# Low weight parts by an accumulating DMA: every fourth ordinary block of a two-layer trunk

## The chip, the cores and the metric

The kernel runs on one NeuronCore of a Trainium2 chip. Five engines work side by side, each through its own queue of instructions in order: TensorE (PE in the profile, its weight loads PEld), VectorE (DVE), ScalarE (ACT), GpSimd (POOL) and SyncE (SP). Sixteen DMA engines move data between DRAM (HBM) and the on-chip memory SBUF. Instructions wait for each other through semaphores.

The metric is the device time of one execution in microseconds (us). The kernel before took 2592.8 us, the median of three runs from 2591.97 to 2593.14.

## The reference

The reference is a decoder trunk with two layers (`DEPTH = 2`), 256 tokens and a width of 2048, in float32. Layer 0 mixes tokens by retention, layer 1 by a short gated convolution; each is followed by a SwiGLU feed-forward part with 5632 hidden columns. Every sub-layer is normalised, scaled and shifted by a conditioning vector, gated and added to the residual:

```python
for i in range(DEPTH):
    mod = (c_act @ w_mod[i] + b_mod[i])[:, None, :]
    sh1, sc1, g1, sh2, sc2, g2 = jnp.split(mod, 6, axis=-1)
    h = (rms_norm(x, norm1_g[i]) * (1.0 + sc1) + sh1).astype(x.dtype)
    ...  # y = retention (layer 0) or short convolution (layer 1) of h
    x = (x + g1 * y).astype(x.dtype)
    h = (rms_norm(x, norm2_g[i]) * (1.0 + sc2) + sh2).astype(x.dtype)
    x = (x + g2 * swiglu(h, ffn_w_in[i], ffn_w_out[i])).astype(x.dtype)
return rms_norm(x, final_g).astype(x.dtype)
```

Nearly all the arithmetic is in the products with `ret_w_in`, `ret_w_out`, `conv_w_in`, `conv_w_out`, `ffn_w_in` and `ffn_w_out`. `w_mod` is large too, but is multiplied by one vector only.

## The kernel before

**Weights as high and low parts.** TensorE multiplies in the format float32r (fp32r), which keeps fewer bits than float32. To hold float32 accuracy, every weight and activation is split into a high part (the value cast to fp32r) and a low part (the value less its high part, cast to fp32r). A product is then the sum of high times high, high times low and low times high. `product` does this with two matmuls for each 128x128 weight tile (L460: the high weight against both parts of the activations, 512 columns; L463: the low weight against the high activations, 256 columns). `by_token` and `thrice` (L473 to L475) do it with three matmuls where weights 512 columns wide are the moving operand.

**Blocks.** All weights, in the order of their use, are laid out on the host in one array `w_all` of 456 blocks, each 128 partitions by 2048 columns (1 MB). `fetch` (L376) loads a block by a DMA from SP into one of three `raw` buffers (`RAW_BUFS = 3`). `prepare` then makes the parts: ScalarE casts each half of 1024 columns to `hi` (L408), VectorE subtracts over all 2048 columns and writes `lo` (L411). The parts go to places of 1024 columns; there are six (`PLACES = 6`), taken in turn, so that three blocks fit. A place can be written again when TensorE has done with it.

Blocks are of three sorts. The first 30 are prepared in halves (pieces 0 and 1). 42 blocks of the last layer belong to a scheme called `Seven`, which computes a 2x2 product of blocks with seven products instead of eight; they are prepared in four pieces (2 to 5) that need differences of weights. The other 384 are ordinary: one piece (6) of 2048 columns. The sevens lie between blocks 335 and 450.

**Modulation.** `w_mod` passes through the same three `raw` buffers: each of 160 later blocks of 1 MB is loaded (L310), multiplied by the conditioning vector and summed by VectorE (L318), and turned into a column by one or two small GpSimd instructions (L323, L325, L328). The sums go through a tile `msum` with four buffers. `paced` spreads these steps over the work until some time in the last layer.

**Order.** TensorE's order is the order of the program (a manual schedule). `take` hands a piece of weights to a matmul and calls `prepare` as long as there is room, that is, while the pieces prepared fit in the six places (`fits`). The order of the other engines' queues is worked out by the framework's scheduler when the kernel is built, with priorities by program order; modulation steps on VectorE have a lower one (`MOD_PRIO`). GpSimd has no other work than the small modulation instructions and a few powers and sums for the norms, and issues no DMA. All loads are issued from SP.

Of the kernel before, what the change touches and what calls it, by code (L numbers as in the profile page):

```python
# [10 lines left out]
F32 = mybir.dt.float32  # L11
# [3 lines left out]
ALU = mybir.AluOpType  # L15
# [33 lines left out]
STEPS = (8, 8, 20)  # L49
RAW_BUFS = 3  # L50
PLACES = 6
LEFT, ENDS, EARLIER = 8, 2, 120

Q0, K0, V0, G0 = 0, HEADS * DK, 2 * HEADS * DK, 2 * HEADS * DK + HEADS * DV
# [202 lines left out]
def trunk(ctx: ExitStack, tc: tile.TileContext, x_in, c_in, pos_in, w_mod, cols_in, gain_in, tab_in, w_all, out):  # L257
    nc = tc.nc
# [104 lines left out]
    for g in groups:  # L363
# [5 lines left out]
    pieces = [  # L369
        (i, p) for i in range(w_all.shape[0])  # L370
        for p in ((2, 3, 4, 5) if i in in_seven else (0, 1) if i < halved else (6,))
    ]

    def fetch():
        raw = wpool.tile([P, CHUNK], F32, tag="raw", name=name("raw"), bufs=RAW_BUFS)
        nc.sync.dma_start(raw, w_all[n_fetched[0]])  # L376
        n_fetched[0] += 1
        fetched.append(raw)

    def prepare(between=None):  # L380
        if prepared[0] == len(pieces):
            return
        _, piece = pieces[prepared[0]]
        prepared[0] += 1
        if piece in (0, 2, 6):
            if not fetched:
                fetch()
            raws[:] = [fetched.pop(0)]
            while first <= units[0] < early and len(fetched) < RAW_BUFS - 1 and n_fetched[0] < w_all.shape[0]:
                fetch()  # L390
        whole = raws[0]
        b = [whole[:, i : i + DV] for i in range(0, CHUNK, DV)]
        raw = whole[:, :HALF] if piece in (0, 4) else whole[:, HALF:] if piece < 6 else whole
        if piece == 2:
            nc.vector.tensor_tensor(differences, whole[:, DV : 3 * DV], whole[:, : 2 * DV], op=ALU.subtract)
        elif piece == 3:
            raw = differences
        elif piece == 4:
            nc.vector.tensor_tensor(b[1], b[2], differences[:, :DV], op=ALU.subtract)
        elif piece == 5:  # L400
            nc.vector.tensor_tensor(b[3], b[3], b[1], op=ALU.subtract)
            raw = b[3]
        width, at = raw.shape[1], HALF * (taken_places[0] % PLACES)
        taken_places[0] += -(-width // HALF)
        hi, lo = [t[:, at : at + width] for t in split_weights]
        steps = [slice(i, min(i + HALF, width)) for i in range(0, width, HALF)]
        for o in steps:
            nc.scalar.copy(hi[:, o], raw[:, o])  # L408
        if between:
            between()  # L410
        nc.vector.tensor_tensor(lo, raw, hi.bitcast(F32), op=ALU.subtract)  # L411
        ready.extend((hi[:, o], lo[:, o], o.stop - o.start) for o in steps)

    taken_places = [0]
    split_weights = [
        wpool.tile([P, PLACES * HALF], F32R, tag=tag, name=tag) for tag in ("hi", "lo")
    ]
    prepared = [0]

    def fits():  # L420
        return prepared[0] < len(pieces) and len(ready) + 1 + (pieces[prepared[0]][1] == 6) <= PLACES

    def take(group, k, col, width=P):

        assert order.pop() == (group, k, col, width)
        i = place[0] or 0
        if i == 0:
            if place[0] == 0:
                ready.pop(0)
            while len(ready) < 1 + AHEAD * (units[0] >= first) or units[0] >= early and fits():  # L430
                n = len(ready)
                prepare()
                if len(ready) == n:
                    break
        place[0] = (i + width) % ready[0][2]
        return [t[:, i : i + width] for t in ready[0][:2]]
# [255 lines left out]
    with ExitStack() as inner:  # L692
# [64 lines left out]
        with tc.tile_pool(name="start", bufs=1) as sp:  # L757
# [59 lines left out]
            with tc.manual_schedule(engines={mybir.EngineType.DVE, mybir.EngineType.Activation}):  # L817
# [61 lines left out]
                def before(k):  # L879
                    low = []  # L880
                    prepare(lambda: low.append(row(k)))
                    low[0]()

                pts = packed(RET_SPANS[0], h, before=before, between=both_reduced, banks=banks)
                prepare()
                prepare()
                for i, pt in enumerate(pts):
# [4 lines left out]
            for k in range(FIRST_KS, KT):  # L892
                steps = ROW_STEPS[k >= SPANS[1][1][1]]
# [557 lines left out]
```

## Time and profile before

| what | value |
|---|---|
| median of three runs | 2592.8 us |
| profiled execution | 2595.2 us |
| its span, first to last instruction | 2593.4 us |
| mean granted TensorE clock | 0.998 |
| DMA | 689.53 MB, mean 266 GB/s |
| loads `raw<-w_all` | 456 of 1024 KB, median 4.9 us to landing |
| loads `raw<-w_mod` | 192 of 1024 KB, median 5.1 us to landing |

How to read the rows: a group is named by line, engine and operation, by what it writes and reads (`out<-in`) and by shape, with its count; then follow its busy time in us and the mean of one in ns, and the idle time of its engine just before it with what ended it. A wait row has the engine that waited, what it waited for, the us in total, the number of waits and the longest. In a row of the timeline the start (us from the start of the span) comes first, then the length. `SPq` is the queue of SP, where DMAs are issued. A DMA row gives the number of transfers, the size of one and the median time from issue to landing; a queue row gives packets, megabytes and the share of the 16 DMA engines' time.

### The profile page before, as it was taken

Reading aid. Unit: us, or ns where it says so; the run is one execution under the profiler, and the core shown is the slowest. Engines: PE = TensorE matmul, PEld = TensorE weight load, DVE = VectorE, ACT = ScalarE, POOL = GpSimd, SP = SyncE. Lnnn points to the kernel's source line nnn. Section 1 sums busy time; section 2 is a strip of 40 time slices with the busy share of each in tenths; the row PEclk is TensorE's granted clock in tenths of the full one; section 3 lists DMA queues with packets and bytes.
Section 4 is the critical chain, followed back from the end, with each engine's and each line's share of the span. In section 5 each row is a group of like instructions: output and inputs, shape, how many; then the busy total and the mean of one; then the engine's idle time right before and its main releaser. Section 6 shows DMA issues by size and latency. Waiting matters only on the chain.

```text
span 2593.4 us, 35836 instructions
## 1 busy us (share of the span) xinstructions
PE 2560.4 (99%) x14181; PEld 2236.5 (86%) x14181; DVE 2167.7 (84%) x2378; ACT 1301.9 (50%) x1792; POOL 158.3 (6%) x232
## 2 busy tenths in 40 slices
PE   7999999999999999999999999999999999999998
PEld 6898889888889888888888898888998888888886
DVE  7988878787698887777777889988988988999877
ACT  5544543444456444334454454444565554555554
POOL 0000000200000000111101200000000000000002
PEclk9999999999999999999999999999999999999999
DMA  9975768767676888778777768887845465455553
GB/s 398 386 309 199 275 239 302 296 260 276 245 284 248 314 335 312 278 306 303 291 299 291 288 248 302 329 304 281 307 155 220 179 234 204 177 213 188 218 200 142
DMA packets 96684, 689.53 MB, mean 266 GB/s; under 512 B 10737, under 2 KB 12161, under 8 KB 13441
## 3 DMA queue, kind: packets, MB, share of 16 engines
q1 hardware_dynamic: 96514, 687.23, 70.4%
q8 instruction: 111, 1.82, 0.3%
q14 instruction: 59, 0.48, 0.1%
HBM read 685.08 MB, written 2.11 MB: 265 GB/s over the span
## 4 chain that ended last, share of the span: by engine, by line
PE 93%; DVE 3%; issue 2%; DMA 1%; ACT 1%; ACTq 0%; POOLq 0%; POOL 0%; DVEq 0%
PE bank L460 29%; PE bank L463 15%; PE bank L473 12%; PE bank L474 12%; PE bank L475 12%; PE bank L509 2%; PE bank L508 2%; PE bank L507 2%; PE bank L640 1%; PE bank L642 1%; PE bank L641 1%; DVE lo L411 1%; DVE raw L768 1%; DMA raw<-w_all 1%; PE bank L996 1%
## 5 line engine op out<-in xcount | busy, mean ns | idle before, releaser
L408 ACT CAST hi<-raw 128x1024 fp32r<-128x1024 f32 (+1 forms) x954 | 968.2, 1032 | 900.2 <-DMA raw<-w_all 344.7
L411 DVE TENSOR_TENSOR lo<-raw,hi 128x2048 fp32r<-128x2048 f32 (+2 forms) x570 | 1078.8, 1901 | 257.8 <-ACT hi L408 256.2
L460 PE MATMUL bank<-h,hi 128*128 128x512 f32 x2016 | 699.2, 390 | 0.0
L463 PE MATMUL bank<-h,lo 128*128 128x256 f32 x2016 | 568.4, 282 | 0.0
L460 PEld LDWEIGHTS bank<-h,hi 128*128 128x128 f32 x2016 | 378.3, 188 | 79.2
L318 DVE SCALAR_TENSOR_TENSOR raw<-raw,cb 128x2048 f32<-128x2048 f32 x160 | 365.9, 2287 | 75.8 <-DMA raw<-w_mod 75.8
L473 PE MATMUL bank<-hi,h 128*128 128x512 f32 x1032 | 404.4, 392 | 2.5 <-DVE rm L752 2.5
L474 PE MATMUL bank<-lo,h 128*128 128x512 f32 x1032 | 402.9, 390 | 0.0
L475 PE MATMUL bank<-hi,h 128*128 128x512 f32 x1032 | 402.1, 390 | 0.0
L463 PEld LDWEIGHTS bank<-h,lo 128*128 128x128 f32 x2016 | 381.0, 189 | 0.0
L460 PE MATMUL bank<-mid,hi 128*128 128x512 f32 x922 | 319.8, 390 | 0.0
L463 PE MATMUL bank<-mid,lo 128*128 128x256 f32 x922 | 260.0, 282 | 0.0
L473 PEld LDWEIGHTS bank<-hi,h 128*128 128x128 f32 x1032 | 194.3, 188 | 40.8 <-DVE rm L752 3.2
L475 PEld LDWEIGHTS bank<-hi,h 128*128 128x128 f32 x1032 | 194.0, 188 | 41.0
L474 PEld LDWEIGHTS bank<-lo,h 128*128 128x128 f32 x1032 | 194.2, 188 | 37.5 <-DVE lo L411 0.3
L460 PEld LDWEIGHTS bank<-mid,hi 128*128 128x128 f32 x922 | 173.0, 188 | 36.3
L463 PEld LDWEIGHTS bank<-mid,lo 128*128 128x128 f32 x922 | 174.3, 189 | 0.0
L460 PE MATMUL bank<-rm,hi 128*128 128x512 f32 x496 | 172.5, 390 | 0.0
L509 PE MATMUL bank<-h,lo 128*128 128x256 f32 x512 | 146.7, 286 | 5.5 <-DVE lo L411 5.5
L507 PE MATMUL bank<-h,hi 128*128 128x256 f32 x512 | 146.2, 286 | 3.5 <-ACT h L796 3.5
L508 PE MATMUL bank<-h,hi 128*128 128x256 f32 x512 | 146.1, 285 | 0.7 <-DVE h L797 0.7
L463 PE MATMUL bank<-rm,lo 128*128 128x256 f32 x496 | 139.8, 282 | 0.0
(256 smaller groups left out, 3230.3 us busy)
## 6 DMA issues: line engine op xcount, KB each, us to landing
raw<-w_all SPq DMA_DIRECT2D x456, 1024.0 KB, 4.9
raw<-w_mod SPq DMA_DIRECT2D x192, 1024.0 KB, 5.1
x<-x_in SPq DMA_DIRECT2D x4, 512.0 KB, 5.4
out<-xt SPq DMA_DIRECT2D x4, 512.0 KB, 3.0
decay<-tab_in SPq DMA_DIRECT2D x8, 128.0 KB, 3.4
x<-gate_row SPq DMA_DIRECT2D x2, 512.0 KB, 4.4
last_gain<-gain_in SPq DMA_DIRECT2D x1, 1024.0 KB
cols<-cols_in SPq DMA_DIRECT2D x1, 152.0 KB, 8.9
```

The costliest lines, as they stand in the source:

```text
L318: nc.vector.scalar_tensor_tensor(raw, raw, 1.0, cb, op0=ALU.mult, op1=ALU.mult, accum_out=total)
L408: nc.scalar.copy(hi[:, o], raw[:, o])
L411: nc.vector.tensor_tensor(lo, raw, hi.bitcast(F32), op=ALU.subtract)
L460: nc.tensor.matmul(pt, hi, h, start=fresh and k == g.ks[0], stop=False, skip_group_check=True)
L463: nc.tensor.matmul(pt[:, 1, :], lo, h[:, 0, :], start=False, stop=last and k == g.ks[-1], skip_group_check=True)
L473: nc.tensor.matmul(o, hi, w_hi, start=first, stop=False)
L474: nc.tensor.matmul(o, hi, w_lo, start=False, stop=False)
L475: nc.tensor.matmul(o, lo, w_hi, start=False, stop=last)
L507: nc.tensor.matmul(pt, hi, h[:, 0, :], start=first, stop=False, skip_group_check=True)
L508: nc.tensor.matmul(pt, hi, h[:, 1, :], start=False, stop=False, skip_group_check=True)
L509: nc.tensor.matmul(pt, lo, h[:, 0, :], start=False, stop=last, skip_group_check=True)
L640: nc.tensor.matmul(pt, hi, high, start=k == 0, stop=False, skip_group_check=True)
```

## The change

For every fourth ordinary block from block 130 on (`index % 4 == 0`, so 132, 136 and so on), VectorE no longer makes the low parts. Instead ScalarE first writes the weights times -1, cast to fp32r, into the place of the low part, for each half of 1024 columns. GpSimd then issues a DMA for each half that reads the same weights once more from `w_all` in DRAM and adds them to what is in the place (`accum_op=ALU.add`): the sum of the weights and the negated high parts is the low part. ScalarE's copies to `hi` come after the two multiplications. 66 blocks are made so, 49 of them up to block 324 and 17 after it, which is 132 multiplications and 132 DMAs. The memory kept in SBUF for descriptors of such DMAs is doubled.

```diff
+ADDED_FROM, ADDED_EVERY = 130, 4
...
     def prepare(between=None):
         if prepared[0] == len(pieces):
             return
-        _, piece = pieces[prepared[0]]
+        index, piece = pieces[prepared[0]]
...
+        by_dma = piece == 6 and index >= ADDED_FROM and index % ADDED_EVERY == 0
         width, at = raw.shape[1], HALF * (taken_places[0] % PLACES)
         taken_places[0] += -(-width // HALF)
         hi, lo = [t[:, at : at + width] for t in split_weights]
         steps = [slice(i, min(i + HALF, width)) for i in range(0, width, HALF)]
+        if by_dma:
+            for o in steps:
+                nc.scalar.mul(lo[:, o], raw[:, o], -1.0)
+                nc.gpsimd.dma_start(lo[:, o], w_all[index, :, o], accum_op=ALU.add)
         for o in steps:
             nc.scalar.copy(hi[:, o], raw[:, o])
         if between:
             between()
-        nc.vector.tensor_tensor(lo, raw, hi.bitcast(F32), op=ALU.subtract)
+        if not by_dma:
+            nc.vector.tensor_tensor(lo, raw, hi.bitcast(F32), op=ALU.subtract)
         ready.extend((hi[:, o], lo[:, o], o.stop - o.start) for o in steps)
...
-    nc = bacc.Bacc("TRN2", target_bir_lowering=False, num_devices=1, dynamic_dma_scratch_size=512)
+    nc = bacc.Bacc("TRN2", target_bir_lowering=False, num_devices=1, dynamic_dma_scratch_size=1024)
```

## The prediction

> **What bounds the kernel now.** I read the busy shares and the chain first, to know the limiting engine.
>
> ```profile
> PE 2560.4 (99%) x14181; PEld 2236.5 (86%) x14181; DVE 2167.7 (84%) x2378; ACT 1301.9 (50%) x1792; POOL 158.3 (6%) x232
> PE 93%; DVE 3%; issue 2%; DMA 1%; ACT 1%; ACTq 0%; POOLq 0%; POOL 0%; DVEq 0%
> ```
>
> TensorE is busy for 99% of the span and carries 93% of the chain. VectorE, which the change relieves, is at 84% and holds 3%. The next view, the busy time by stretches (columns: window and length, then busy us and count for each engine, granted clock, DMA share, GB/s), shows where the idle remainder lies.
>
> ```profile
> core 0: us, PE busy (x) PEld busy (x) DVE busy (x) ACT busy (x) POOL busy (x), PEclk, DMA share, GB/s
> 0.00:64.80 64.80, 49.68 (x250) 39.39 (x251) 49.80 (x58) 35.70 (x59) 1.58 (x5) 1.00 0.97 398
> 785.00:1858.00 1073.00, 1073.00 (x6396) 959.99 (x6395) 879.93 (x954) 512.15 (x741) 107.57 (x144) 1.00 0.79 295
> 1935.00:2570.00 635.00, 633.97 (x2834) 524.28 (x2833) 568.58 (x597) 355.34 (x408) 10.36 (x2) 1.00 0.54 199
> ```
>
> Block 132, the first that is changed, is used at about 785 us. From there to 1858 us TensorE is busy in all 1073.0 us; in the last layer it lacks 1.0 us of 635. Its waits after 785 us are one row:
>
> ```profile
> PE bank L473 <- DVE mid L1349: 1.0, 2, 0.5
> ```
>
> None is for a low part (`lo`). So a freer VectorE has about 1 us to win. What counts is whether the new way of making `lo` stays ahead of TensorE, and what it does to the loads. The groups, DMA rows and waits of 785 to 1858 us carry that:
>
> ```profile
> L411 DVE TENSOR_TENSOR lo<-raw,hi 128x2048 fp32r<-128x2048 f32 x193 | 441.8, 2289 | 98.5 <-ACT hi L408 97.7
> L408 ACT CAST hi<-raw 128x1024 fp32r<-128x1024 f32 x386 | 399.9, 1050 | 409.7 <-DMA raw<-w_all 231.6 <-PE bank L460 136.7 <-PE bank L463 14.5
> L318 DVE SCALAR_TENSOR_TENSOR raw<-raw,cb 128x2048 f32<-128x2048 f32 x109 | 249.3, 2287 | 65.2 <-DMA raw<-w_mod 65.2
> q1 hardware_dynamic: 43388, 315.87, 78.5%
> raw<-w_all SPq DMA_DIRECT2D x193, 1024.0 KB, 4.9
> raw<-w_mod SPq DMA_DIRECT2D x109, 1024.0 KB, 4.9
> ACT hi L408 <- DMA raw<-w_all: 231.6, 108, 5.8
> SPq L376 <- DVE lo L411: 179.9, 52, 8.2
> ```
>
> The reader should see two things. The 302 loads take 0.785 x 1073 = 842 us of all DMA engines, 2.79 us each. And ScalarE's copy waits for a load 108 times: there no loaded block lies in reserve, because the three `raw` buffers go straight from use to the next load (the last row: SP waits for L411 to free one).
>
> **The change part by part.**
>
> *Removed.* 66 subtractions on VectorE: blocks 132, 136 ... without those of the sevens, 49 of them to block 324 and 17 after. 66 x 2.289 = 151 us of VectorE, beside TensorE throughout; worth 0, at most the 1.0 us above.
>
> *Added on ScalarE.* 132 multiplications over 128x1024. No such row exists; the copy of the same shape takes 1.05 us (ends 1.0 and 1.1, nothing speaks for more), so 139 us in all. In the first stretch ScalarE goes from 512 to 512 + 98 x 1.05 = 615 of 1073 us: covered by its own idle time. But they stand ahead of the high copies, which come 2.1 us later; `raw` is freed after four ScalarE instructions (4.2 us) where it was after two copies and L411 (2.1 + 2.3 us). So the buffer gains nothing, and the high copies still finish within the lead worked out now.
>
> *The lead.* One block's rows, by time (start, length):
>
> ```profile
> 968.11 0.39 PE L460 MATMUL bank<-h,hi 128*128 128x512 f32 x1
> 971.23 0.39 PE L460 MATMUL bank<-h,hi 128*128 128x512 f32 x1
> 974.52 2.00 ACT L408 CAST hi<-raw 128x1024 fp32r<-128x1024 f32 x2
> 985.32 0.28 PE L463 MATMUL bank<-h,lo 128*128 128x256 f32 x1
> 2234.16 1.06 ACT L408 CAST hi<-raw 128x1024 fp32r<-128x1024 f32 x1 [0.30 <-PE bank L475]
> 2242.99 0.39 PE L474 MATMUL bank<-lo,h 128*128 128x512 f32 x1
> ```
>
> From 968.11 to 971.23 are nine tiles, 0.347 us each; eight make a half-block, 2.77 us. There are six half places, so the lead from a place coming free to its use is at most 5 x 2.77 = 13.9 us. Block 164 (third and fourth row) has 10.8 us, as its load sets its start. In the last layer, where sevens stand ahead and use their places up faster, block 392 (last two rows) has 8.8 us. After one multiplication the first half's addition has 9.8 us (7.8 in the last layer); the second half's starts 1.05 us later and is used 2.77 later: 11.5 (9.5).
>
> *Added on GpSimd: 132 DMA issues.* The trace has no DMA issued there. The nearest rows are its small instructions:
>
> ```profile
> 1046.38 0.29 POOL L323 TENSOR_SCALAR mcol<-msum,cols 128x1 f32<-128x1 f32 x1 [4.98 <-DVE raw L318]
> 1060.09 2.26 POOL L323 TENSOR_SCALAR mcol<-msum,cols 128x1 f32<-128x1 f32 x1 [13.15 <-DVE raw L318]
> 1059.91 2.29 DVE L411 TENSOR_TENSOR lo<-raw,hi 128x2048 fp32r<-128x2048 f32 x1
> ```
>
> The same instruction takes 0.29 us alone and 2.26 us when L411 started just before it: it ends with L411. So an issue costs 0.3 to 2.3 us. I take 0.3, because L323 reads a tile through GpSimd and an issue doesn't.
>
> [...]
>
> *The addition itself, in DMA time.* A block moves 1 MB from DRAM, reads 1 MB of `lo` and writes 1 MB. Ends: one load's price, 2.79 us, if the second read is free; three, 8.4 us, if each stream costs as much as a load. A saving isn't possible, since the loads all stay. I take two, 5.58 us: a load has one stream on the reading side, this has two. Then 49 x 5.58 = 273 us, or 0.255 of the stretch, and the demand is 0.785 + 0.255 = 1.04: 43 us more than there is. At the pace of the first slices (398 GB/s at share 0.97, so 2.56 us a load) the same 302 + 98 loads' worth takes 1024 us and just fits. Between 0 and 43 us I take 30, nearer the end that is priced in the stretch itself, since three buffers can't keep the queue full and no loaded block is in reserve. With a late load, the next blocks' copies and L411 are late, then TensorE.
>
> [...]
>
> *Its latency.* A load lands 4.9 us after issue, so 2.1 us beside its 2.79 us of transfer; two other rows of the profile bound that part:
>
> ```profile
> out<-xt SPq DMA_DIRECT2D x4, 512.0 KB, 3.0
> gate_row<-row SPq DMA_DIRECT2D x1, 8.0 KB, 3.4
> ```
>
> 3.0 - 1.4 = 1.6 us, and at most 3.4 us. I take 2.1. A half's addition then takes 0.3 + 2.1 + 2.79 x 1.79 (loads share the engines) = 7.4 us of its 9.8; the second, behind the first, 7.4 + 5.0 - 1.05 = 11.3 of 11.5: just in time, with 0.2 us left. In the last layer, at share 0.54: 6.7 of 7.8, and 6.7 + 4.3 - 1.05 = 9.9 of 9.5, late by 0.4 us: 17 x 0.4 = 7 us. With one stream both halves have us to spare; with three the second is late by 4.8 us in each block.
>
> *Queue order.* GpSimd works in order, and nearly always stands at a wait:
>
> ```profile
> POOL g L328 <- DVE raw L318: 417.1, 46, 37.6
> POOL mcol L323 <- DVE raw L318: 291.4, 32, 42.0
> POOL s L328 <- DVE raw L318: 252.6, 32, 10.9
> ```
>
> That is 961 of 1073 us in front of a modulation step. An addition queued behind such a step waits for its L318; in turn a modulation step behind an addition waits for ScalarE's multiplication, and L318 only after four more (four `msum` buffers), which costs nothing. I take 0 for the first in the sum and keep it as a rival. SP's queue gets nothing new; the doubled descriptor memory costs 0 (an SBUF reserve, no instruction).
>
> *Sum.* 0 + 30 + 7 = 37 us. The profiled execution took 2595.2 us (span 2593.4), so 2632; the median, 2592.8, is 2.4 us lower: 2630.
>
> **The rivals.**
>
> *Hidden, not slower.* The second read is nearly free: demand 0.785 + 49 x 2.79 / 1073 = 0.91, latencies well inside the lead. It decides where a block costs less than (0.97 - 0.785) x 1073 / 49 = 4.05 us, 1.45 loads. For it speaks that share 0.97 did occur; against it the two reads and the 108 waits for loads. Time 2593 (2591 to 2597).
>
> *Three streams.* Demand 0.785 + 0.382 = 1.17, 179 us too much (76 us at 2.56 a load); the late second halves, 4.8 x 49 = 235 us, largely overlap. About 2760, from 2680. Against it: writing and reading go on together in a load too.
>
> *Issued late, behind modulation steps.* One step per 1073 / 109 = 9.8 us; an issue stuck behind one waits 4.9 us in the mean, so the first half needs 12.3 of 9.8 us. If half of the 49 are caught, 25 x 2.5 = 61 us more: about 2690. Issues held by L411, 2.0 us each, give the like: 49 x 1.8 = 88 us if all are held, and the chance counts both. For it speak the 961 us; against it that additions and steps follow the same loads in order.
>
> *Faster.* It would need more than the 1 us of TensorE's waits; the rows have no place for it.
>
> **How the numbers follow.** 0.2% (5.2 us) is about what a measurement of this kernel can tell from no change. Forecast 0.45 (own range 2599 to 2677: 43 us, and the last 17 blocks held by 2 us more); hidden 0.27; three streams 0.13; behind modulation steps 0.12; faster 0.03. So faster 0.03, same 0.27, slower 0.70. The range 2590 to 2740 takes in the hidden case, the forecast and most of the fourth, and leaves out most of the third.
>
> **What would show it.** L411 of 128x2048 at 318 where 384 were; 132 new ScalarE rows of 1.05 us; a second DMA queue whose share gives the price (5.6 us a block, 14% of the span); DMA share over 0.95 between 785 and 1900 us; loads landing in 6 us or more; TensorE waiting for a DMA into `lo`, or for `hi` behind late loads, some 30 us before 1900 and few after. I am wrong if that queue costs under 4 us a block and TensorE stays at full busy; or if additions land within 5 us of issue yet are issued late, since then GpSimd's queue is the cause.

## The result and the profile after

The changed kernel takes 2822.3 us, the median of four runs (2813.6 to 2827.7), against 2593.0 us (2592.0 to 2594.1): a ratio of 1.0879, with a 95% interval from 1.0865 to 1.0894. That is 229 us more, where 37 were forecast. The profiled execution took 2821.8 us, its span 2820.1 us. (The change adds lines, so L408 becomes L414, L411 becomes L418, L460 and L463 become L467 and L470, L473 to L475 become L480 to L482 and L318 becomes L319; the multiplication is L411 now and the addition L412.)

From the page of the kernel after: busy times, queues, the chain, two groups and the DMA rows.

```profile
PE 2641.2 (94%) x14181; PEld 2279.9 (81%) x14181; DVE 2033.1 (72%) x2312; ACT 1409.3 (50%) x1924; POOL 275.1 (10%) x364
...
q1 hardware_dynamic: 96514, 687.23, 64.5%
q0 software_dynamic: 19008, 69.21, 13.4%
...
PE 38%; DMA 32%; issue 12%; DVE 12%; ACT 5%; POOL 0%; DVEq 0%; ACTq 0%; SPq 0%; POOLq 0%
DMA raw<-w_mod 13%; DMA raw<-w_all 11%; PE bank L481 7%; PE bank L482 7%; PE bank L480 7%; DMA lo<-w_all 7%; DVE lo L418 6%; PE bank L467 4%; ACT hi L414 3%; DVE raw L319 3%; PE bank L470 2%; PE bank L515 2%; PE bank L516 2%; PE bank L514 2%; ACT lo L411 1%
...
L412 POOL DMA_DIRECT2D lo<-w_all x132 | 117.1, 892 | 945.1 <-ACT lo L411 818.0
...
L411 ACT ACTIVATE lo<-raw 128x1024 fp32r<-128x1024 f32 x132 | 138.9, 1057 | 57.1 <-DMA raw<-w_all 54.6
...
raw<-w_all SPq DMA_DIRECT2D x456, 1024.0 KB, 5.5
raw<-w_mod SPq DMA_DIRECT2D x192, 1024.0 KB, 6.0
lo<-w_all POOLq DMA_DIRECT2D x132, 512.0 KB, 10.4
```

TensorE falls from 99% to 94% and from 93% to 38% of the chain; DMAs, which had 1% of it, have 32%: 24% are loads and 7% additions. Queue q0 is that of the additions: 13.4% of 2820.1 us is 378 us, 5.7 us for each of 66 blocks. VectorE is busy 135 us less, and it does not matter.

TensorE's two largest waits in the kernel after:

```profile
PE bank L470 <- DMA lo<-w_all: 108.7, 59, 5.4
PE bank L481 <- DMA lo<-w_all: 30.7, 14, 3.4
```

Both are for an addition to land; L470 uses the low weights in layer 0 and L481 in the last layer. The busy time by stretches, for the changed blocks up to 324 and for the last layer:

```profile
core 0: us, PE busy (x) PEld busy (x) DVE busy (x) ACT busy (x) POOL busy (x), PEclk, DMA share, GB/s
785.00:2000.00 1215.00, 1104.71 (x6239) 969.23 (x6238) 756.26 (x875) 574.16 (x814) 188.23 (x234) 0.96 0.89 294
2150.00:2820.00 670.00, 628.25 (x2739) 512.26 (x2738) 518.53 (x562) 362.82 (x424) 43.55 (x36) 0.98 0.62 205
```

The DMA share is 0.89, not over 0.95, while TensorE lacks 110 us of 1215: on average the DMA engines are not full, and TensorE waits for DMAs all the same. Its clock is lower too. The timeline behind one wait shows what that is (start, length, instruction, idle time before it):

```profile
1013.64 0.58 PE L470 MATMUL bank<-h,lo 128*128 128x256 f32 x1 [3.70 <-DMA lo<-w_all]
1014.02 0.63 PE L467 MATMUL bank<-h,hi 128*128 128x512 f32 x1
1014.45 0.41 PE L470 MATMUL bank<-h,lo 128*128 128x256 f32 x1
1014.66 0.63 PE L467 MATMUL bank<-h,hi 128*128 128x512 f32 x1
```

After 3.70 us of waiting the matmuls take 0.63 and 0.41 us, where the prediction's rows have 0.39 and 0.28. The granted clock in the trace is one half from 1012.3 us, during the wait, for 6.83 us; most of these stretches last 3.41 us. Before has two stretches at half clock (11.5 us in all, both outside the parts looked at here), after has 35 (144 us). Of the 81 waits over 0.3 us that come after 200 us, 34 have such a stretch beside them, the shortest clear case a wait of 1.6 us; one of 2.8 us has none.

The matmuls are the same 14181 in the same order in both kernels, so each can be set against its fellow: the growth of the distance from one matmul's start to the next, summed, gives the loss by stretch, and growths under 0.3 us are matmuls that merely run slower. In this way 174 us are lost from 785 to 1858 us of before's time (124 us in waits, 50 us in slow matmuls) and 51 us in the last layer (38 and 13). The rest, 4 us, lies between. "Loss" below is always this reading, and "landing" is the mean time from issue to landing of the loads from block 132 to block 324 (5.2 us before, 7.4 us after; the trace has the landing of 264 of these 302). Both are of the profiled execution, while times are medians of the runs; the two differ by up to 12 us.

Other waits of the kernel after, on the engines behind:

```profile
POOL lo L412 <- ACT lo L411: 818.0, 78, 60.8
...
ACT hi L414 <- DMA raw<-w_all: 614.2, 182, 11.6
...
DVE raw L319 <- DMA raw<-w_mod: 179.8, 62, 8.3
```

GpSimd mostly stands waiting for the multiplication when it comes to an addition. The issue starts 0.4 us after its multiplication ends in the median, and 12 of 132 start more than 1 us after it (at most 2.3 us), so additions are hardly ever stuck behind modulation steps. ScalarE and VectorE wait for loads far more than before: over the whole span, the second row had 344.7 us in 166 waits and the third 75.8 us in 50.

### The profile page after: what moved, and what is told of

It is laid out like the page before. It is cut to its first block, busy times and chain, and to the rows that moved or that the text cites. A ratio compares the mean times of both kernels' runs of the same rounds, so it can differ in the third digit from the quotient of the medians.

```text
span 2820.1 us, 36286 instructions
## 1 busy us (share of the span) xinstructions
PE 2641.2 (94%) x14181; PEld 2279.9 (81%) x14181; DVE 2033.1 (72%) x2312; ACT 1409.3 (50%) x1924; POOL 275.1 (10%) x364
## 3 DMA queue, kind: packets, MB, share of 16 engines
q0 software_dynamic: 19008, 69.21, 13.4%
## 4 chain that ended last, share of the span: by engine, by line
PE 38%; DMA 32%; issue 12%; DVE 12%; ACT 5%; POOL 0%; DVEq 0%; ACTq 0%; SPq 0%; POOLq 0%
DMA raw<-w_mod 13%; DMA raw<-w_all 11%; PE bank L481 7%; PE bank L482 7%; PE bank L480 7%; DMA lo<-w_all 7%; DVE lo L418 6%; PE bank L467 4%; ACT hi L414 3%; DVE raw L319 3%; PE bank L470 2%; PE bank L515 2%; PE bank L516 2%; PE bank L514 2%; ACT lo L411 1%
## 5 line engine op out<-in xcount | busy, mean ns | idle before, releaser
L414 ACT CAST hi<-raw 128x1024 fp32r<-128x1024 f32 (+1 forms) x954 | 961.1, 1029 | 1037.0 <-DMA raw<-w_all 614.2
L418 DVE TENSOR_TENSOR lo<-raw,hi 128x2048 fp32r<-128x2048 f32 (+2 forms) x504 | 928.1, 1851 | 347.0 <-ACT hi L414 343.0
L467 PE MATMUL bank<-h,hi 128*128 128x512 f32 x2016 | 729.5, 402 | 0.0
L470 PE MATMUL bank<-h,lo 128*128 128x256 f32 x2016 | 587.0, 291 | 73.1 <-DMA lo<-w_all 73.0
L319 DVE SCALAR_TENSOR_TENSOR raw<-raw,cb 128x2048 f32<-128x2048 f32 x160 | 366.2, 2289 | 214.1 <-DMA raw<-w_mod 179.8
L470 PEld LDWEIGHTS bank<-h,lo 128*128 128x128 f32 x2016 | 395.6, 196 | 87.4 <-DMA lo<-w_all 87.1
L467 PEld LDWEIGHTS bank<-h,hi 128*128 128x128 f32 x2016 | 393.2, 195 | 83.3
L481 PE MATMUL bank<-lo,h 128*128 128x512 f32 x1032 | 406.8, 394 | 22.1 <-DMA lo<-w_all 20.1
L480 PE MATMUL bank<-hi,h 128*128 128x512 f32 x1032 | 407.6, 395 | 2.0 <-DVE rm L759 2.0
L482 PE MATMUL bank<-hi,h 128*128 128x512 f32 x1032 | 405.0, 392 | 0.0
L467 PE MATMUL bank<-mid,hi 128*128 128x512 f32 x922 | 331.1, 400 | 0.0
L470 PE MATMUL bank<-mid,lo 128*128 128x256 f32 x922 | 267.2, 290 | 36.0 <-DMA lo<-w_all 35.7
L481 PEld LDWEIGHTS bank<-lo,h 128*128 128x128 f32 x1032 | 195.9, 190 | 65.2 <-DMA lo<-w_all 24.4
L482 PEld LDWEIGHTS bank<-hi,h 128*128 128x128 f32 x1032 | 195.6, 190 | 41.4
L480 PEld LDWEIGHTS bank<-hi,h 128*128 128x128 f32 x1032 | 195.6, 190 | 40.9 <-DVE rm L759 2.7
L470 PEld LDWEIGHTS bank<-mid,lo 128*128 128x128 f32 x922 | 179.5, 195 | 42.5 <-DMA lo<-w_all 41.9
L412 POOL DMA_DIRECT2D lo<-w_all x132 | 117.1, 892 | 945.1 <-ACT lo L411 818.0
L467 PEld LDWEIGHTS bank<-mid,hi 128*128 128x128 f32 x922 | 178.4, 194 | 37.8
L467 PE MATMUL bank<-rm,hi 128*128 128x512 f32 x496 | 172.5, 390 | 0.0
L411 ACT ACTIVATE lo<-raw 128x1024 fp32r<-128x1024 f32 x132 | 138.9, 1057 | 57.1 <-DMA raw<-w_all 54.6
L516 PE MATMUL bank<-h,lo 128*128 128x256 f32 x512 | 146.5, 286 | 4.5 <-DVE lo L418 4.5
L514 PE MATMUL bank<-h,hi 128*128 128x256 f32 x512 | 146.1, 285 | 3.3 <-ACT h L803 3.3
## 6 DMA issues: line engine op xcount, KB each, us to landing
lo<-w_all POOLq DMA_DIRECT2D x132, 512.0 KB, 10.4
```

The lines of the kernel that those rows point to most:

```text
L319: nc.vector.scalar_tensor_tensor(raw, raw, 1.0, cb, op0=ALU.mult, op1=ALU.mult, accum_out=total)
L411: nc.scalar.mul(lo[:, o], raw[:, o], -1.0)
L412: nc.gpsimd.dma_start(lo[:, o], w_all[index, :, o], accum_op=ALU.add)
L467: nc.tensor.matmul(pt, hi, h, start=fresh and k == g.ks[0], stop=False, skip_group_check=True)
L470: nc.tensor.matmul(pt[:, 1, :], lo, h[:, 0, :], start=False, stop=last and k == g.ks[-1], skip_group_check=True)
L480: nc.tensor.matmul(o, hi, w_hi, start=first, stop=False)
```

## The experiments

Two causes were on trial. **Traffic**: the additions' packets delay the loads, and late loads make everything behind them late. **Lateness**: an addition takes longer than its lead, whatever the loads do. Each kernel is set against before on the same chip. (Most expectations call lateness theory 1 or L, and traffic theory 2, or R where it acts through the ring of three buffers. Of the labels that they use, e2_traffic and e11_traffic_only are the kernels with traffic alone, with and without the multiplications, e8_fourth_raw is the change with a fourth buffer, e13_chain the first chain and e5_first_half the first kernel without a second half.)

**The parts without their size.** Every mechanism of the change stays, but only 128 of 1024 columns are added.

```diff
-                nc.gpsimd.dma_start(lo[:, o], w_all[index, :, o], accum_op=ALU.add)
+                part = slice(o.start, o.start + P)
+                nc.gpsimd.dma_start(lo[:, part], w_all[index, :, part], accum_op=ALU.add)
```

> Only the first 128 of the 1024 columns of each half are added, so seven eighths of these low parts hold the negated high part alone; the 132 multiplications, the 132 issues and every wait stay. Theory 1 (TensorE waits because a half's addition takes 8.9 and 11.8 us from issue to landing, against a lead of about 11.6 us that 1.5 us are spent on before the issue): some 4 us of transfer go from each, TensorE no longer waits, 2593 to 2600 us, and the granted clock is back at 0.998. Theory 2 (the additions' transfers crowd out the loads): an eighth of the traffic, also 2593 to 2600. Theory 3 (the multiplications ahead of the copies, or GpSimd's queue, make the parts late): nothing of that is changed, still 2780 to 2825.

Measured: 2592.6 us, ratio 1.0006 [0.9994, 1.0017]. Loss 2 us in the first stretch, landing 5.6 us. From its page:

```profile
q0 software_dynamic: 19008, 8.66, 2.8%
...
lo<-w_all POOLq DMA_DIRECT2D x132, 64.0 KB, 5.6
```

So 132 multiplications, 132 issues and the waits as such cost nothing; bytes or time of the additions do.

**A copy in the addition's place** (`accum_op` left out) moves the same bytes with one stream less.

> The DMA copies the weights over the low part's place instead of adding them, so these low parts hold the whole weight; it still waits for the multiplication and TensorE for it. The DMA reads one stream, so a block takes some 2.8 us of all engines instead of 5.7, and each half lands some 2 to 4 us sooner. Theory 1: the second half lands at about 11 us after the first multiplication begins, used at 14.3: no waits or few, 2593 to 2620. Theory 2: half of the added traffic, so up to half of the loss, 2600 to 2710. If it is the issue by GpSimd and not the second stream that makes the landing late: 2780 or more.

Measured: 2677.2 us (two runs), ratio 1.0324 [1.0303, 1.0344]; losses 72 and 13 us in the first stretch and the last layer, landing 6.4 us. Its queue:

```profile
q0 software_dynamic: 19008, 69.21, 8.0%
```

8.0% of its span of 2676.4 us is 214 us, 3.2 us a block against 5.7: a DMA that adds costs 1.8 times a copy. A little over half the price (3.2 of 5.7) costs 84 of the 229 us. A half also lands sooner here (5.8 us after its issue in the median for a first half, 8.9 us for a second, against 8.3 and 11.4 us), so this run doesn't tell the two causes apart.

**Traffic alone.** VectorE makes all low parts again; for blocks 132 to 320 ScalarE multiplies into a spare tile, the DMAs add there, and nobody reads it.

```diff
-                nc.scalar.mul(lo[:, o], raw[:, o], -1.0)
-                nc.gpsimd.dma_start(lo[:, o], w_all[index, :, o], accum_op=ALU.add)
+                spare = spares[0].tile([P, HALF], F32R, tag="spare", name=name("spare"), bufs=2)
+                nc.scalar.mul(spare, raw[:, o], -1.0)
+                nc.gpsimd.dma_start(spare, w_all[index, :, o], accum_op=ALU.add)
```

> VectorE makes every low part as before the change; for the 48 blocks from 132 to 320 ScalarE also multiplies into a spare tile and GpSimd's DMA adds the weights to it, and nothing reads the spare tile. So the traffic, the multiplications and the issues are there, without anyone waiting for the additions. Theory 1 (latency): TensorE hardly waits, 2593 to 2605. Theory 2 (traffic): the loads are crowded out as the prediction had it, at least 30 us slower, 2623 to 2750.

Measured: 2753.8 us, ratio 1.0606 [1.0585, 1.0627], loss 156 us, landing 6.9 us, DMA share 0.90. Two kernels take this apart: one has a multiplication of a single column before each addition, the other has the multiplications and no DMA.

> As e2_traffic, 48 blocks, but without the multiplications: the DMA adds the weights to two spare tiles again and again, started by a multiplication of a single column; nobody reads them, and raw is held no longer than before the change. Theory R (the ring of three raw buffers has no reserve: each of the 302 loads between 785 and 1858 us that lands 1 us later costs 302 / 3, about 100 us in all): the mean landing rises by 1.2 to 1.7 us, as in e2_traffic, and the time to 2690 to 2760. If e2_traffic lost its 161 us through the multiplications, which hold raw for 2.1 us more: 2593 to 2630.

> As e2_traffic, 48 blocks, but without the DMAs: ScalarE multiplies into the spare tile ahead of its copies and VectorE makes every low part. Theory R: 48 loads hold their buffer 2.1 us longer, 0.33 us in the mean of 302, at most 33 us: 2593 to 2626. If the multiplications were the cause of e2_traffic's loss: 2700 or more.

Measured: 2746.5 us (1.0591 [1.0575, 1.0606], loss 146 us, landing 7.0 us) with the DMAs alone, and 2593.9 us (1.0002 [0.9992, 1.0011]) with the multiplications alone. TensorE's largest wait with the DMAs alone:

```profile
PE bank L470 <- DVE lo L418: 89.8, 48, 6.0
```

Nobody needs these additions, and TensorE waits for VectorE's low parts of ordinary blocks. Traffic alone, 3.0 us a block, costs nearly as much as the change does in this stretch. The DMA records show what the loads lose: in the kernel after, additions have packets under way in 37% of the time from 785 to 2000 us, and then loads hold 7.0 of the 16 engines in the mean (by the time of their packets), against 12.9 at other times.

**Half as many blocks** (every eighth, into spare tiles):

> The additions into a spare tile that nobody reads, as in e2_traffic, for every eighth block from 136 to 320: 24 blocks. Theory 2 with a filling of 0.90: 842 + 24 x 5.7 = 979 us of DMA work takes 1088 us, 15 us over the 1073: 2600 to 2620 us. A loss in proportion to the number of blocks would be half of e2_traffic's 161: 2673. Theory 1: 2593.

Measured: 2669.2 us, ratio 1.0293 [1.0278, 1.0309], loss 70 us, landing 6.1 us, DMA share 0.85. Half the blocks give half the loss, with 15% of the DMA time unused. Were the limit a demand above what the engines can move, as the prediction had it, half the additions (0.785 + 0.13 = 0.91) would have been free.

**Less traffic from elsewhere.** In the change, modulation loads only half of each block (VectorE goes over that half twice; this leaves out half of the sums).

```diff
-            nc.vector.scalar_tensor_tensor(raw, raw, 1.0, cb, op0=ALU.mult, op1=ALU.mult, accum_out=total)
+            for c in (cb[:, :HALF], cb[:, HALF:]):
+                nc.vector.scalar_tensor_tensor(a, a, 1.0, c, op0=ALU.mult, op1=ALU.mult, accum_out=total)
```

> The changed kernel with each of the 160 later modulation loads cut to its first 1024 columns; VectorE runs over these twice, so the modulation sums are not those of the reference and VectorE's time stays about the same. Theory 2 (between 785 us and the last layer the DMA engines, filled to 0.90, are the limit): their work there falls from 842 + 273 to 690 + 273 = 963 us, at 0.90 some 1070 us, which fits the 1073; the loss of 174 us there falls to 0 to 40, and with the 51 us of the last layer the time is 2640 to 2690. Theory 1 (the additions' latency alone): the waits stay, 2770 to 2825.

Measured: 2805.7 us, ratio 1.0827 [1.0806, 1.0847]; losses 161 and 40 us, DMA share 0.80, landing 6.7 us. Before had a share of 0.79. The additions stay as they were here, and so does most of the loss: the mean fill of the engines is not what decides.

**A fourth buffer.** Every fourth load goes to a fourth `raw` buffer, up to block 314; in the change, and with the traffic alone.

> The changed kernel with a fourth raw buffer while blocks 130 to 314 are fetched (every fourth load of weights or modulation goes to it). If three buffers are what keeps the DMA engines at 0.90 (theory 2a), the share rises to 0.95 or more and the first stretch's loss of 174 us falls to 60 to 110: 2700 to 2760 us. If the engines can give no more with both queues in use (theory 2b), or if the additions' latency is what counts (theory 1), it stays at 2800 to 2825.

> e11_traffic_only with the fourth raw buffer of e8_fourth_raw. Theory R (the ring of three has no reserve): with a fourth buffer a load may land some 3.5 us later before it is missed, so most of the 153 us go: 2595 to 2650 us. If the DMA engines themselves are the limit: 2720 to 2750.

Measured: 2778.1 us (1.0716 [1.0698, 1.0734], losses 123 and 43 us, landing 8.0 us) and 2715.3 us (1.0472 [1.0456, 1.0487], loss 116 us, landing 7.4 us). The DMA shares are 0.91 and 0.92, and both times lie between what the two readings gave. With three buffers, a load can be issued only as one comes free: three periods of the loads are one landing plus the time the buffer is held. Before, 3 x 3.56 = 10.7 us, of which 5.2 are landing and the remainder, 5.5, is holding. With the traffic alone it is 3 x 4.07 = 12.2 us, 7.0 and 5.2: the longer landing would explain the slower turn. That reading would have a fourth buffer win back nearly all; it wins 44 of 229 and 31 of 153 us. So the turn of the buffers is a part at most. That single late loads do the rest is read from places like this one, in the fourth-buffer kernel with traffic alone (L327 is the modulation step, L426 the subtraction, L478 the matmul with the low weights):

```profile
1348.27 2.29 DVE L327 SCALAR_TENSOR_TENSOR raw<-raw,cb 128x2048 f32<-128x2048 f32 x1 [7.08 <-DMA raw<-w_mod]
...
1350.83 2.28 DVE L426 TENSOR_TENSOR lo<-raw,hi 128x2048 fp32r<-128x2048 f32 x1
...
1353.17 0.58 PE L478 MATMUL bank<-h,lo 128*128 128x256 f32 x1 [4.25 <-DVE lo L426]
```

VectorE stands 7.08 us for a modulation load, the subtraction comes behind that step in its queue, and TensorE waits 4.25 us for the subtraction.

**Who passes a late load on.** Followed back from TensorE's 48 waits over 0.3 us in the first stretch with the traffic alone (99.5 us in all), 26 (57.8 us) go through a modulation step that stood for its load and 21 (40.0 us) through ScalarE's standing for a weight load. So VectorE's stand was taken away: the modulation step reads only `cb`, and a one-column GpSimd instruction waits for the load in its place.

```diff
-            nc.vector.scalar_tensor_tensor(raw, raw, 1.0, cb, op0=ALU.mult, op1=ALU.mult, accum_out=total)
+            nc.vector.scalar_tensor_tensor(cb, cb, 1.0, cb, op0=ALU.mult, op1=ALU.max, accum_out=total)
...
-            nc.gpsimd.tensor_tensor(dst, total, b, op=ALU.add)
+            nc.gpsimd.tensor_tensor(dst, total, raw[:, :1], op=ALU.add)
```

> The kernel with the traffic alone (48 blocks' additions into spare tiles, low parts all by VectorE, 2746.5 us), but VectorE's modulation step reads only the conditioning tile, so that it no longer waits for its load; the load stays, and a one-column GpSimd instruction waits for it and for the step, which holds the buffer. The modulation values are left out by this. Theory 1: in the trace of the traffic alone, 26 of 48 waits of TensorE (57.8 of 99.5 us), followed back, pass through a modulation step that stood for a late load of w_mod with subtractions queued behind it; 21 waits (40 us) pass through ScalarE's copy standing for a late load of w_all. Then 153 us of loss go to 153 x 40 / 99.5 = 62 us: 2655 us, from 2635 to 2690, and the waits that are left pass through ScalarE. Rival: the loads as such are late, and what VectorE no longer waits for ScalarE waits for: 2725 to 2750.

> The same edit in the kernel after (2822 us); the modulation values are left out by it. Theory 1: 58 of the 60 waits of the first stretch there end with an addition that lands, and no addition waits for VectorE, so little is won: 2790 to 2825. Rival: the standing modulation steps also make the additions late, as 18 of the 60 waits (38 of 114 us), followed back past the addition, end at a load of w_mod: then about a third of the 174 us goes, 2765 us, from 2740 to 2785.

Measured: 2757.4 us (1.0637 [1.0619, 1.0655]) with the traffic alone, and 2809.3 us (1.0832 [1.0816, 1.0848]) in the change. The first theory falls for the traffic: no gain where 90 us were expected. Waits of the traffic kernel so changed, on ScalarE and TensorE:

```profile
ACT hi L415 <- DMA raw<-w_all: 542.9, 160, 14.1
...
PE bank L470 <- DVE lo L418: 91.7, 44, 5.8
```

Followed back, 30 of the 49 waits over 0.3 us there (47.8 us) now go through ScalarE's standing for a weight load, and at least 14 (39.9 us) still end at a modulation load by way of GpSimd, mostly because VectorE's step then waits for one of the four `msum` buffers:

```profile
DVE cb L319 <- POOL s L329: 53.7, 26, 6.7
DVE cb L319 <- POOL g L329: 47.3, 25, 7.2
```

What one queue does not wait for, the next does. In the change the edit brings 13 us, as the first theory had it for that kernel; all 62 waits over 0.3 us of its first stretch end with an addition.

**Lateness alone.** Each half's addition is replaced by a chain of tiny ones (16 partitions, 128 columns) on the same tile, which are slow one after another and move almost nothing. The first kernel has three links for the first half and four for the second, the others two and three, and two and two. They leave out most of the addition.

```diff
-                nc.gpsimd.dma_start(lo[:, o], w_all[index, :, o], accum_op=ALU.add)
+            for links in range(4):
+                for o in steps[links // 3 :]:
+                    part = slice(o.start, o.start + P)
+                    nc.gpsimd.dma_start(lo[:16, part], w_all[index, :16, part], accum_op=ALU.add)
```

> The changed kernel with each half's addition replaced by a chain of three (first half) or four (second half) additions over 16 partitions and 128 columns, each waiting for the one before it; so the parts come some 9 to 13 us after their first issue with hardly a byte moved, and most of these low parts hold the negated high part alone. Theory L (TensorE waits for additions that land after their use): 1 to 3 us of wait and clock in each of the 66 blocks, 2650 to 2800 us, with loads landing as before. Theory R alone: 2593 to 2605.

> e13_chain with two links for the first half and three for the second, so about 9.5 and 13 us from first issue to last landing, 1 to 2 us over the changed kernel's 8.3 and 11.4; most of these low parts hold the negated high part alone. Theory L as the main cause: a loss of the changed kernel's size or more, 2780 to 2900 us. Theory R as the main cause: clearly less than the change's 228 us, most of it in the last layer, 2620 to 2740.

> e13_chain with two links for each half: about 9.5 us for both, 1 us over the changed kernel's first half and 2 us under its second; most of these low parts hold the negated high part alone. The lead for the second half is 14.3 us, of which 4 go before its issue, so it is in time; the first half has 11.6 less 1.5: 10.1 us. Theory L with these leads: few waits, 2595 to 2640 us. If late additions cost more than the leads say: 2700 or more.

| links | first issue of a half to last landing, median us, first and second half | time, us | ratio | loss, first stretch / last layer, us |
|---|---|---|---|---|
| 2, 2 | 9.7, 10.0 | 2634.5 | 1.0159 [1.0142, 1.0176] | 28 / 18 |
| 2, 3 | 9.6, 13.7 | 2899.4 | 1.1180 [1.1152, 1.1207] | 235 / 61 |
| 3, 4 | 14.4, 17.8 | 3157.4 | 1.2172 [1.2150, 1.2194] | 448 / 103 |
| the change | 8.3, 11.4 | 2822.3 | 1.0879 [1.0865, 1.0894] | 174 / 51 |

From the page of the kernel with three and four links:

```profile
q0 software_dynamic: 14784, 3.81, 1.2%
...
raw<-w_all SPq DMA_DIRECT2D x456, 1024.0 KB, 4.8
```

And from its waits:

```profile
PE bank L473 <- DMA lo<-w_all: 280.4, 75, 8.9
```

Loads land as before (5.2 to 5.4 us in the mean in all three kernels), and TensorE waits: a late addition costs by itself, with three and four links more than was expected. The edge is sharp. From 10.0 to 13.7 us for the second half, 207 us are added over 49 blocks, 4.2 us a block. The change's 11.4 us lies between; a straight line there gives about 105 us for the first stretch, which is an estimate and not a measurement.

**Only the last layer** (`ADDED_FROM = 325`, 17 blocks):

> The change in the last layer alone, in the 17 blocks from 328 on, where the DMA share before was 0.54. In the changed kernel this part lost 51 us. If that is the latency of the additions (second half 10.9 us after its issue, three microseconds after the first), the loss stays though no load is crowded out: 2635 to 2650 us, with waits for the DMA into lo and none for loads. If it came from the congestion before it: 2593 to 2605.

Measured: 2643.5 us, ratio 1.0191 [1.0176, 1.0206], loss 0 and 48 us. One row of its waits, then two of its DMA rows:

```profile
PE bank L481 <- DMA lo<-w_all: 29.3, 13, 3.3
```

```profile
raw<-w_all SPq DMA_DIRECT2D x456, 1024.0 KB, 4.9
...
lo<-w_all POOLq DMA_DIRECT2D x34, 512.0 KB, 8.8
```

Traffic is low there, loads keep their 4.9 us, and TensorE waits 13 times in the 17 blocks. A first half lands 7.1 us after its issue and a second 10.6 us.

**No second half.** In every second ordinary block, the first half by DMA and the second by VectorE: as many additions, none queued behind another. The second kernel has the fourth buffer too.

> Every second ordinary block has its first half made by the DMA and its second half by VectorE: 131 multiplications and 131 additions of 512 KB, against 132 of each, but never two behind each other. Theory 1: a first half lands 8.9 us after issue or a little sooner, 10.4 us after its multiplication begins, against a lead of 11.6 in the median and 10.0 at the lower end: waits in few blocks, 2595 to 2650, well under half of the loss. Theory 2: the same traffic, the same loss, 2780 or more. Theory 3: the same number of multiplications and issues, 2780 or more.

> e5_first_half with the fourth raw buffer of e8_fourth_raw: the traffic of the change, but no addition behind another and a ring with reserve. Theories R and L together: the first stretch loses less than in either (151 and 123 us), 2600 to 2680 us. If something else keeps TensorE waiting: 2740 or more.

Measured: 2752.3 us (1.0611 [1.0586, 1.0636], losses 151 and 8 us, landing 7.2 us) and 2711.8 us (1.0453 [1.0437, 1.0468], losses 110 and 4 us, landing 7.7 us). Both times lie between the ranges expected. Most of the last layer's loss goes, as lateness has it: a single addition lands in 6.8 us there (median), and 1 of 32 is late. The first stretch's stays. An addition lands in 8.1 us there though none is ahead of it, and 42 of 99 land after TensorE is ready for them. These are the largest waits in the kernel with three buffers:

```profile
PE bank L473 <- DMA lo<-w_all: 94.3, 38, 5.8
```

## Why the prediction was wrong

The direction was right, the size was not: 229 us instead of 37, and past the upper end of the range.

*Right.* The freed VectorE gains nothing. The multiplications take 1.06 us each (138.9 us) and cost nothing, as the kernel with 48 blocks' multiplications alone shows. The price of an addition was taken as two streams, 5.58 us a block; it is 5.7. A packet of 4096 B takes 327 ns in the additions' queue, 174 ns there in the kernel that copies, and 159 ns in SP's queue (medians; the weight loads' own packets are 8192 B and take 309 ns). So an adding packet takes 2.06 times as long as one of SP's queue (327 / 159), and 1.88 times as long as a copied one. GpSimd's queue order, a rival, plays hardly any part, and the issues aren't held: their rows take 0.86 to 1.19 us in the changed kernel, and the 19 that start while a subtraction of VectorE runs at most 0.92. In two other kernels one issue each took over 3 us (3.30 us in e2_traffic), right behind a small GpSimd instruction that itself took 2.7 and 2.9 us beside VectorE's work.

*Wrong: the DMA term, "between 0 and 43 us I take 30".* The amount of work was right. The loads and additions of the stretch were to take 842 + 273 = 1115 us of all engines; the trace has 301 x 4.14 x 0.889 = 1108. The step from work to time failed. It set the demand against the capacity of the whole stretch, as if a load could be late without harm as long as the mean fits. Traffic alone, with as good as the same price, costs 146 to 156 us at a share of 0.90, where the step took 30; half of it costs 70 us at 0.85, where the step gives nothing. An addition comes as a burst that leaves the loads in flight 7.0 engines instead of 12.9. That with three buffers and no loaded block in reserve a late load then makes the next ones late is argued from the waits; the fourth buffer won back a fifth only. The prediction had the row for that, ScalarE's 108 waits for a load, and used it only to choose a value between 0 and 43.

*Wrong: the latency term, "7.4 us of its 9.8; the second 11.3 of 11.5: just in time".* The durations were near. From its issue, a first half lands in 8.3 us and a second in 11.4 us in the median (95% of them within 11.1 and 14.1; the medians of the first stretch are 8.9 and 11.6); the 11.3 us of the prediction are counted from the second half's own issue too. Of the 8.3 us, 0.9 is the issue, and the first packet starts 3.1 us after the issue's start. What failed for the second half is the lead. The prediction let the second issue follow 1.05 us behind the first; in the trace of the first stretch it follows 2.7 us behind (median), since ScalarE mostly does other work between. So the second half lands 15.8 us after the start of the first multiplication, and TensorE is ready for it after 14.9 us: 39 of 49 are late, by 1.1 us in the median of all 49, not early by 0.2. For the first half the duration was too short by 1.5 us and its spread was missing: it was to be 2.4 us early, lands after 10.6 us with TensorE ready after 10.4 us, and 22 of 49 are late. In the last layer "17 x 0.4 = 7 us" is 48 to 51 us: 13 of the 17 second halves are late, 13 waits of 2.2 us in the mean, and slow matmuls add 13 us.

*Missing: the clock.* Beside many waits of 1.6 us and more the clock is one half for 3.41 us, in six cases for 6.83 us. The matmuls that run slower in such a stretch cost 1.1 to 1.8 us, and 2.3 to 2.7 us in the long ones. That is 63 of the 229 us (50 and 13), and no step had it. What sets such a stretch off isn't shown: waits as short as 1.6 us had one, and one of 2.8 us had none. Before has one of 3.41 us too, from 129.7 us, beside waits of 1.8 and 0.8 us, and I should have priced the expected waits with such stretches.

*What stays open.* Traffic alone costs about 150 us in the first stretch, and lateness alone, by the chains, between 28 and 235 (about 105 by the straight line); together they cost 174, so they overlap, and no run splits it. In the change 58 of some 60 waits over 0.3 us there end with an addition, 37 times a second half and 21 times a first, with about 55.5 us for either. Traffic works in part through these late additions: in 28 of the 58 waits (54 us) the block's first multiplication had itself stood waiting for its weight load, in 30 (57 us) it had not. With the traffic alone it works by another way, VectorE's low parts, and the second addition follows the first at a shorter distance (0.6 to 1.0 us against 2.7), so its 150 us is not the traffic's part of the 174. That the bursts, rather than something else about a second DMA queue, are what delays the loads is read from the engines' shares; single halves in twice as many blocks lose 151 us in that stretch, and no run has spread one addition out.

No kernel here beats before: TensorE was full, and what comes level (the multiplications alone, an eighth of the columns) has left out what costs.

## What to carry to other kernels

A transfer that TensorE will wait for needs its lead set against the slow cases of its landing, from the instruction that truly starts it, and not against a median (here 8.3 us for a first half, and 11.1 us for 95% of them). A mean DMA share under 1 does not say that more traffic is free (here half the blocks' additions cost 70 us at a share of 0.85): look for engines that already wait for loads (here 108 waits in 1073 us, three buffers) and price what each burst does to the loads in flight. And where a tensor engine runs without a break, add to every new wait of some microseconds what the slow matmuls at half clock may cost (here 1.1 to 2.7 us a stretch, beside 34 of 81 waits).

## What the runs showed of the hardware

- A DMA that adds costs 5.7 us of all sixteen engines for 1 MB, a copy by the same queue 3.2 us and a plain load 2.8 us; packets of 4096 B take 327 ns (adding), 174 ns (copying) and 159 ns (SP's queue).
- An adding DMA issued by GpSimd takes that engine 0.88 us and a copying one 0.55 us (medians); the first packet of a first half starts 3.1 us after the start of the issue. A chain of two tiny ones (8 KB each) on one tile takes 9.7 us, so one dependent step costs almost 5 us; a single first half of 64 KB lands in 4.7 us.
- While additions run, loads hold 7.0 of 16 engines in the mean instead of 12.9 (the kernel after, 785 to 2000 us). The order in which one engine takes the packets of the two queues isn't in these traces.
- Beside the wait of 3.70 us shown above, TensorE's clock was one half for 6.83 us, 5.5 of them after the wait; beside most waits that have such a stretch it was 3.41 us. Waits as short as 1.6 us had one, and one of 2.8 us had none.
